# A two-layer attention trunk: memory's normalization factor is applied behind the key and value products

## The chip, the cores and the metric

The kernel runs on one core of a Trainium2 chip. The core has five engines with a queue each: TensorE (PE, matrix products; its loads of the stationary operand are shown as PEld), VectorE (DVE), ScalarE (ACT), GpSimd (POOL) and SyncE (SP, which issues most transfers). An engine works through its queue in order and waits on semaphores for the others. The metric is the time of one execution on the device in microseconds (us), as the median of several. Before the change it is 966.31 us (three runs, 966.08 to 968.67).

## The reference

The reference is a trunk of two layers over 512 tokens of width 1024, with 256 memory tokens of the same width. The part that matters here is the attention into memory, which each layer does with its own weights over the same memory:

```python
def rmsnorm(x, g):
    xf = x.astype(jnp.float32)
    y = xf * lax.rsqrt(jnp.mean(xf * xf, axis=-1, keepdims=True) + EPS)
    return (y * g.astype(jnp.float32)).astype(x.dtype)
...
    mem_h = rmsnorm(mem, mem_norm_g[i])
...
    kv = jnp.einsum('bnd,de->bne', mem_h, w_kv).reshape(Bn, N, 2, MEM_HEADS, HEAD_DIM)
    k = rmsnorm(kv[:, :, 0], kn_g)
    v = kv[:, :, 1]
```

A row of `mem` is divided by its root mean square (one number per memory token, here called its factor), multiplied by a row of 1024 gains, and multiplied with the weights of key and value. The keys are normalized once more, per head of 128. `x` goes through an `rmsnorm` of its own in each layer, and then through a wide input projection, a token mixer (dilated windows in layer 0, grouped queries in layer 1), the memory attention, a gate, and an output projection that is added to `x`.

## The kernel before

**Products in three parts.** Each f32 operand is split into a high part in the rounded format of TensorE (`wh` for weights, `act`, `h` for activations; ScalarE copies it) and the rest (`wo`; VectorE subtracts it, L305 and L161). A product is high times high and low times high (L170, L171, `mm_early`), then high times low weights (L174, `mm_late`). Four blocks of 128 rows give eight early and four late products, called a group.

**Weights.** `Weights` holds the loads in one list in the order of use. `W.dma` issues loads of 512 KB on SP while buffers are free, `W.hi` makes ScalarE's copy (L295), `W.lo` VectorE's subtraction (L305). Four buffers each of `wh` and `wo` turn round.

**Order.** The program is written out by hand: Python calls issue each instruction onto its engine's queue. A `Driver` holds side tasks as generators: after each group of products `drv.tick` lets those run a step that are due. `chunk` runs groups: it takes the weights, calls `group` for each block of rows, then frees banks, advances the weights and ticks. So side tasks stand behind the group that was issued just before.

**The start (from L885).** SP loads memory's gain row (4 KB), x's gain row (4 KB), two blocks of memory (512 KB each) with weights between, the gain columns, and four blocks of x with more weights. TensorE spreads both gain rows over the 128 partitions by multiplying a column of ones with them (`row_bank`, L606): four products, two passes each. The squares of a memory block run on ScalarE and, for one half of the first block, VectorE (`norm_1`); POOL adds them, adds epsilon and raises to −1/2 (L477, L436, L437). VectorE multiplies by factor and gain row (`norm_2`, L482). TensorE transposes four squares of 128 (`turn4`, L488), ScalarE copies the high part, VectorE subtracts the low one. `mid` puts a small product (`busy`) and work on the weights between. `ahead`, called ahead of each group, transposes the remaining quarters of memory and copies x's gain row from its bank.

**Key and value (`mem_kv`).** Two `proj_t` chunks: keys with two units of weights by two blocks of memory tokens, then values. The keys' `ev_k` squares the heads on ScalarE (L573), takes the factor per head on POOL (L436, L437), multiplies on VectorE (L578), transposes (L585) and writes both parts (L633, L634). The values' `ev_v` writes both parts with a constant 0.5 (L656, L657). Beside the keys and values the side task `prep` normalizes and transposes x: `norm_1` on ScalarE and POOL, L482 on VectorE, L488 on TensorE, copies and differences for the products of the first large projection, which follows.

**The second layer.** `mem_norm(1)` is a side task during the output projection of layer 0. It loads memory again, computes the factor again, scales and transposes. `mem_kv(1)` follows the output projection, while the new x is normalized.

## Time and profile before

| what | value |
|---|---|
| median of three runs | 966.31 us |
| the profiled execution | 968.3 us |
| its span, first to last instruction | 966.5 us |
| TensorE busy | 946.8 us, 98% |
| VectorE busy | 791.4 us, 82% |
| ScalarE busy | 681.7 us, 71% |
| GpSimd busy | 341.4 us, 35% |
| mean granted TensorE clock | 0.996 |

The numbers come from one execution that the hardware profiler recorded. Times in its rows are us from the start of the span. A row of the timeline has start, duration, engine, source line, operation, output and inputs with their shapes, a count when several are merged, and in brackets how long the engine had stood idle and what ended that. A row of the chain of waits has start, duration, and what the chain consists of there. A row of the windows has the stretch, its length, then busy us with the number of instructions for PE, PEld, DVE, ACT and POOL, the granted TensorE clock, the busy share of the transfer engines and GB/s. A row of the groups has the shape, the busy us in all, and the mean ns of one.

### The profile page before, as it was taken

The page shows a single profiled execution, that of the slowest core. Times are in us where ns is not written, and L with a number is a line of the kernel's source. Part 1 is how long each engine was busy: PE and PEld are TensorE (multiplying, and loading weights), DVE is VectorE, ACT ScalarE, POOL GpSimd, SP SyncE. Part 2 cuts the span into 40 slices and gives each one's busy share as a digit, 9 for nine tenths or more (in the row PEclk, how much of TensorE's full clock was granted, in tenths as well). Part 3 has the DMA queues.
Part 4 walks back from the last instruction along what each step waited for, and adds up shares of the span by engine and source line. Part 5 has one row for each costly group of instructions (what it writes and reads, how often), then busy time and mean ns, then how long its engine had stood idle before and what let it go on. Part 6 is the DMA issues. An engine that isn't in the chain of part 4 may idle for free.

```text
span 966.5 us, 16604 instructions
## 1 busy us (share of the span) xinstructions
PE 946.8 (98%) x5682; PEld 833.2 (86%) x5682; DVE 791.4 (82%) x1411; ACT 681.7 (71%) x1701; POOL 341.4 (35%) x482
## 2 busy tenths in 40 slices
PE   8999999999999999999999999999899999999998
PEld 5879888888888888888899997788899999998886
DVE  5898676878888888888888999769878898769883
ACT  5775689686868686868685657546768977879770
POOL 1512423557554545454726011322332330111010
PEclk9999999999999999999999999999899999999999
DMA  9989956969686868685959889889766687777744
GB/s 360 317 235 327 271 116 172 294 120 268 149 258 143 262 150 258 154 261 132 283 132 241 266 206 297 268 242 366 167 157 129 199 235 179 207 204 190 206 131 131
DMA packets 89129, 209.81 MB, mean 217 GB/s; under 512 B 25298, under 2 KB 36050, under 8 KB 89044
## 3 DMA queue, kind: packets, MB, share of 16 engines
q1 hardware_dynamic: 69892, 145.76, 43.4%
q0 software_dynamic: 17856, 60.83, 33.4%
q10 hardware_dynamic: 1296, 2.16, 0.6%
q8 instruction: 45, 0.74, 0.3%
q14 instruction: 40, 0.33, 0.1%
HBM read 157.27 MB, written 12.65 MB: 176 GB/s over the span
## 4 chain that ended last, share of the span: by engine, by line
PE 80%; DVE 8%; DMA 6%; ACT 3%; issue 2%; POOL 1%; SPq 0%; DVEq 0%; POOLq 0%; ACTq 0%
PE pj L170 21%; PE pj L171 21%; PE pj L174 20%; DVE wo L305 2%; PE qT L585 2%; PE sa L1106 1%; PE oo L1208 1%; PE pt L1187 1%; PE sa L1102 1%; PE ptb L1405 1%; DMA og<-odb 1%; DMA acc<-sn 1%; DMA wl<-wl 1%; DMA grB<-in_qn_b_dram 1%; DMA od<-o 1%
## 5 line engine op out<-in xcount | busy, mean ns | idle before, releaser
L305 DVE TENSOR_TENSOR wo<-wl,wh 128x1024 fp32r<-128x1024 f32 x255 | 315.1, 1242 | 6.0 <-ACT wh L295 5.8
L295 ACT CAST wh<-wl 128x1024 fp32r<-128x1024 f32 x255 | 268.5, 1060 | 29.3 <-PE pj L171 18.9
L170 PE MATMUL pj<-wh,hS 128*128 128x512 f32 (+1 forms) x448 | 159.0, 368 | 3.9 <-DVE sn L389 3.9
L171 PE MATMUL pj<-wh,hS 128*128 128x512 f32 (+1 forms) x448 | 153.6, 356 | 0.0
L170 PE MATMUL pj<-wh,h 128*128 128x512 f32 (+1 forms) x336 | 117.9, 365 | 0.0
L171 PE MATMUL pj<-wh,h 128*128 128x512 f32 (+1 forms) x336 | 114.0, 353 | 0.0
L437 POOL TENSOR_TENSOR rstd<-mse,half 128x4 f32<-128x4 f32 (+2 forms) x98 | 103.1, 1052 | 8.2
L174 PE MATMUL pj<-wo,hS 128*128 128x512 f32 (+1 forms) x448 | 100.8, 355 | 2.0 <-DVE wo L305 2.0
L170 PEld LDWEIGHTS pj<-wh,hS 128*128 128x128 f32 x448 | 85.9, 192 | 14.8 <-issue 2.6
L171 PEld LDWEIGHTS pj<-wh,hS 128*128 128x128 f32 x448 | 86.1, 192 | 10.3
L372 ACT COPY sn<-pj 128x512 f32<-128x512 f32 x132 | 73.1, 590 | 29.7 <-PE pj L174 29.7
L436 POOL TENSOR_SCALAR mse<-hss 128x4 f32<-128x4 f32 (+1 forms) x86 | 45.1, 525 | 132.2 <-ACT junk L573 128.0
L174 PEld LDWEIGHTS pj<-wo,hS 128*128 128x128 f32 x448 | 75.3, 191 | 14.5 <-DVE wo L305 2.7
L573 ACT ACTIVATE junk<-sn 128x128 f32<-128x128 f32 x264 | 79.1, 308 | 4.1 <-DVE sn L383 4.1
L1050 POOL TENSOR_TENSOR ta<-sn,tabs 128x128 f32<-128x128 f32 (+1 forms) x64 | 37.4, 592 | 118.6 <-DVE sn L578 92.0
L389 DVE TENSOR_TENSOR sn<-pj,sn 128x512 f32<-128x512 f32 x99 | 67.7, 686 | 12.3 <-PE pj L174 11.8
L174 PE MATMUL pj<-wo,h 128*128 128x512 f32 (+1 forms) x336 | 74.8, 352 | 0.0
L171 PEld LDWEIGHTS pj<-wh,h 128*128 128x128 f32 x336 | 63.8, 190 | 7.4
L170 PEld LDWEIGHTS pj<-wh,h 128*128 128x128 f32 x336 | 63.6, 189 | 7.4 <-DVE sn L389 0.2
L279 POOL DMA_DIRECT2D wl<-wl x33 | 29.1, 881 | 111.9 <-DVE wo L305 56.0
L174 PEld LDWEIGHTS pj<-wo,h 128*128 128x128 f32 x336 | 56.0, 189 | 8.7
L578 DVE TENSOR_TENSOR sn<-sn,rstd 128x512 f32<-128x512 f32 (+1 forms) x82 | 48.0, 594 | 7.2 <-POOL rstd L437 7.2
(235 smaller groups left out, 2335.1 us busy)
## 6 DMA issues: line engine op xcount, KB each, us to landing
wl<-in_wall_dram SPq DMA_DIRECT2D x222, 512.0 KB, 7.0
wl<-wl POOLq DMA_DIRECT2D x66, 512.0 KB, 5.5
wl<-in_wall_dram POOLq DMA_DIRECT2D x42, 512.0 KB, 8.5
acc<-sn POOLq DMA_DIRECT2D x16, 256.0 KB, 4.8
od<-o SPq DMA_DIRECT2D x12, 256.0 KB, 5.6
og<-od SPq DMA_DIRECT2D x12, 256.0 KB, 5.5
odb<-o SPq DMA_DIRECT2D x12, 256.0 KB, 3.4
og<-odb SPq DMA_DIRECT2D x12, 256.0 KB, 4.2
```

The costliest lines, as they stand in the source:

```text
L170: T.matmul(o, a, b, start=start, stop=False, skip_group_check=True)
L171: T.matmul(o, c, d, start=False, stop=False, skip_group_check=True)
L174: T.matmul(o, a, b, start=False, stop=stop, skip_group_check=True)
L295: A.copy(wh, self.tile[self.items[i]])
L305: V.tensor_tensor(wo, self.tile[key], wh.bitcast(F32), ALU.subtract)
L372: A.copy(t, b)
L389: V.tensor_tensor(t, b, t, ALU.subtract if q == "12" else ALU.add)
L436: G.tensor_scalar(e, ss, EPS, None, ALU.add)
L437: G.tensor_tensor(r, e, half[:, 0:n], ALU.pow)
L573: A.activation(jk, p[:, j * 128:(j + 1) * 128], AF.Square, scale=QS, accum_out=ss[:, j:j + 1])
L578: V.tensor_tensor(xn[:, 0:n], p.rearrange("p (a b) -> p a b", a=4)[:, 0:n], r[:, 0:n, None].to_broadcast([128, n, 128]), ALU.mult)
L1050: G.tensor_tensor(ta[:, 0:n], xn[:, 0:n, 0:32], ropeA[:, 0, b, s0:s0 + n], ALU.mult)
```

## The change

Memory's rows are multiplied by the gain row alone and transposed; the factor of a row is applied behind the products, where each memory token is a partition again. Three columns hold it: the factor itself, the factor times 128^-1/2 for the squares of the key heads, and half of it for the values. For the keys, the head factor from POOL is multiplied once more (`G.tensor_scalar(r, r, rm[0]...)`), since the product lacks the row's factor. Layer 1 uses the columns that layer 0 left, since memory is the same, and computes no squares.

x's gain row is no longer spread by TensorE and copied by ScalarE, but loaded to all 128 partitions by a transfer of 512 KB. One product of a row of zeros (`idle`, `IDLE = 1`) stands ahead of memory's row products, and the small product `busy` is gone. The order of the first loads changes: two weight loads between the memory blocks.

The hook that `proj_t` calls moves from ahead of a group (`pre`) to between its early and late products (`mid`), and what `ahead` does moves a group earlier. The high part of the very first transposed quarter is copied by VectorE.

```diff
-    def proj_t(act, sels, evac, pre=None):
+    def proj_t(act, sels, evac, mid=None):
         def group(w, u, b, p):
             for k in range(4):
                 kk = 4 * u + k
                 mm_early(p, sels[b](act, 0, kk), w[k][0], sels[b](act, 1, kk), w[k][0], kk == 0)
+            if mid:
+                mid(u, b)
             for k in range(4):
...
-    def head_sq(p, n=4):
+    def head_sq(p, n=4, by=QS):
...
-            A.activation(jk, p[:, j * 128:(j + 1) * 128], AF.Square, scale=QS, accum_out=ss[:, j:j + 1])
+            A.activation(jk, p[:, j * 128:(j + 1) * 128], AF.Square, scale=by, accum_out=ss[:, j:j + 1])
...
+    def mem_mul(xb, row, j):
+        t = s2(name="mg")
+        V.tensor_tensor(t, xb[j], row[j], ALU.mult)
+        return t
+    def mem_turn(M, t, b, j):
+        cs = slice(b * 128, (b + 1) * 128)
+        turn4(t, M.block(0, j, cs), M.block(1, j, cs))
+    def mem_factor(b, ss):
+        e = sm(1, "mse")
+        G.tensor_tensor(e, ss[:, 0:1], ss[:, 1:2], ALU.add)
+        r = rstd_of(e, 1)
+        for k, by in enumerate((1.0, QS, 0.5)):
+            G.tensor_scalar(rm[k][:, b:b + 1], r, by, None, ALU.mult)
+    def mem_rows(layer):
...
         yield MEM_D
-        n = [norm_1(t[0])]
-        yield 1
-        n.append(norm_1(t[1]))
-        norm_2(t[0], n[0], rows["m"])
-        yield 1
-        norm_2(t[1], n[1], rows["m"])
         M = Act(NM)
         for b in range(2):
+            g = [mem_mul(t[b], rows["m"], j) for j in range(2)]
+            yield 1
             for j in range(2):
-                norm_3(t[b], M, b * 128, j)
+                mem_turn(M, g[j], b, j)
             yield 1
...
-            r = head_sq(p)
+            r = head_sq(p, by=rm[1][:, b:b + 1])
             def rest():
+                G.tensor_scalar(r, r, rm[0][:, b:b + 1], None, ALU.mult)
                 xn = head_mul(p, r)
...
-            A.activation(vt_[0][:, b], p, AF.Copy, scale=0.5)
-            V.scalar_tensor_tensor(vt_[1][:, b], p, 0.5, vt_[0][:, b].bitcast(F32), ALU.mult, ALU.subtract)
+            A.activation(vt_[0][:, b], p, AF.Copy, scale=rm[2][:, b:b + 1])
+            V.scalar_tensor_tensor(vt_[1][:, b], p, rm[2][:, b:b + 1], vt_[0][:, b].bitcast(F32), ALU.mult, ALU.subtract)
...
-    for b in range(2):
-        nc.sync.dma_start(mt[b], mem[b * 128:(b + 1) * 128])
-        W.dma(1)
+    nc.sync.dma_start(mt[0], mem[0:128])
+    W.dma(2)
+    nc.sync.dma_start(mt[1], mem[128:256])
     W.dma(2)
...
         nc.sync.dma_start(xt[c], xv[c])
+        if c == 0:
+            row_load("x", norm_g[0:1, :])
...
-    first = row_bank("m0", WARM)
-    gain = row_bank("x0", 1, pj)
...
+    idle = tabs[0:1, 512:1024]
+    V.memset(idle, 0.0)
+    for n in range(IDLE):
+        T.matmul(at("idle"), ones, idle, start=True, stop=True)
+    first = row_bank("m0")
...
+    mg = {(0, 0): mem_mul(mb[0], first, 0)}
+    square(0, 0)
+    square(0, 1, True)
+    p = turn4(mg[0, 0], None, None)
+    hi, lo = M.block(0, 0, slice(0, 128)), M.block(1, 0, slice(0, 128))
+    split(hi, lo, p, False)
     W.hi(True)
+    W.lo()
     W.hi(True)
-    norm_2(mb[1], nst[1], first, (0,))
+    mg[1, 0] = mem_mul(mb[1], first, 0)
     W.lo()
+    mem_factor(0, ss[0])
     def ahead(u, b):
+        if (u, b) == (0, 0):
+            mem_turn(M, mg[1, 0], 1, 0)
+            for c in range(2):
+                mg[c, 1] = mem_mul(mb[c], first, 1)
+                square(1, c)
+            mem_factor(1, ss[1])
         if (u, b) == (0, 1):
-            for j in range(2):
-                A.copy(rows["x"][j], gain[j])
-            norm_3(mb[1], M, 128, 0)
             for c in range(2):
-                norm_2(mb[c], nst[c], first, (1,))
-        if (u, b) == (1, 0):
-            for c in range(2):
-                norm_3(mb[c], M, 128 * c, 1)
+                mem_turn(M, mg[c, 1], c, 1)
...
-    drv.spawn(mem_norm(1), MEM_B)
+    drv.spawn(mem_rows(1), MEM_B)
```

In the queues this gives, after the first low operand: on ScalarE the two weight casts of the second unit of the keys and the first squares of x now stand behind the last two copies of memory's transposed quarters; on POOL the extra multiplication for the first key block stands behind the norm of the third x block, that for the second behind the fourth's.

More of the change, by code (lines that the diff above doesn't have):

```diff
@@ L27 @@
 MEM_D = 4
+IDLE = 1
 PD = 2
@@ L944, in setup, with square @@
             yield 1
[L946 to L964 removed]
+    idle = tabs[0:1, 512:1024]
[3 more added lines that the diff above has]
+    first = row_bank("m0")
+    mb, M = [halves(t) for t in mt], Act(NM)
+    ss = [sm(2, "ss") for _ in range(2)]
+    def square(b, j, vector=False):
+        jk = s2(name="sq")
+        if vector:
+            V.tensor_tensor_reduce(jk, mb[b][j], mb[b][j], 1.0 / 1024.0, 0.0, ALU.mult, ALU.add, ss[b][:, j:j + 1])
+        else:
+            A.activation(jk, mb[b][j], AF.Square, scale=1.0 / 32.0, accum_out=ss[b][:, j:j + 1])
+    mg = {(0, 0): mem_mul(mb[0], first, 0)}
[4 more added lines that the diff above has]
+    split(hi, lo, p, False)
+    W.hi(True)
+    W.lo()
     W.hi(True)
[L966 removed]
+    mg[1, 0] = mem_mul(mb[1], first, 0)
     W.lo()
+    mem_factor(0, ss[0])
     def ahead(u, b):
+        if (u, b) == (0, 0):
[4 more added lines that the diff above has]
+            mem_factor(1, ss[1])
         if (u, b) == (0, 1):
[L972 to L974 removed]
             for c in range(2):
[L976 to L979 removed]
+                mem_turn(M, mg[c, 1], c, 1)
     drv.spawn(prep(), PD)
```

27 lines of the change are left out of this document (6 added, 21 removed).

## The prediction

> **What bounds the kernel.** I read the page first, then the chain of waits in order of time, then the timeline of each engine where the change works, the windows, and the groups by form.
>
> ```profile
> span 966.5 us, 16604 instructions
> PE 946.8 (98%) x5682; PEld 833.2 (86%) x5682; DVE 791.4 (82%) x1411; ACT 681.7 (71%) x1701; POOL 341.4 (35%) x482
> ...
> 2.26 7.16 PE row L606 x8
> 9.41 1.04 PE xT L488 x4
> ...
> 11.18 0.75 PE pj L170
> ...
> 12.65 0.43 PE pj L170
> ...
> 14.36 0.25 PE pj L170
> ```
>
> TensorE is busy 98% of the span, so nothing between the two ends of the change can give time. What can give or cost is where TensorE stands: the start (first product at 11.18, eight passes of row products, 7.16 us, ahead of it) and the places where another engine sets its pace. A product takes 0.43 us at 12.65 and 0.25 from 14.36 on: the clock comes up at about 14.3.
>
> ```profile
> 31.00:40.00 9.00, 9.00 (x51) 7.72 (x50) 9.00 (x13) 6.86 (x20) 5.47 (x7) 1.00 0.90 314
> 50.00:60.00 10.00, 9.78 (x42) 7.51 (x42) 9.84 (x15) 8.67 (x13) 2.29 (x3) 1.00 0.93 175
> ...
> 29.85 1.29 DVE L161 TENSOR_TENSOR h<-xT,h 128x512 fp32r<-128x512 f32 x2 [1.00 <-ACT h L158]
> 61.85 0.68 DVE L389 TENSOR_TENSOR sn<-pj,sn 128x512 f32<-128x512 f32 x1
> 62.59 0.50 PE L170 MATMUL pj<-wh,hS 128*128 128x512 f32 x1 [1.43 <-DVE sn L389]
> ```
>
> In the windows (behind the length stand TensorE, its loads, VectorE, ScalarE and POOL) VectorE has no gap from 31 on. At 62.59 TensorE stands 1.43 us for it. So TensorE's lead at the start is spent there: the time at 62.59 is that of VectorE's queue, which began at 29.85, when ScalarE had copied the first transposed x block.
>
> ```profile
> 16.72 2.00 ACT L295 CAST wh<-wl 128x1024 fp32r<-128x1024 f32 x2
> 18.62 0.63 ACT L475 ACTIVATE sq<-x 128x512 f32<-128x512 f32 x1
> 20.89 1.08 ACT L158 CAST act<-xT 128x512 fp32r<-128x512 f32 x2 [0.93 <-PE xT L488]
> 21.85 2.01 ACT L295 CAST wh<-wl 128x1024 fp32r<-128x1024 f32 x2
> 23.75 0.64 ACT L475 ACTIVATE sq<-x 128x512 f32<-128x512 f32 x1
> 25.08 0.28 ACT L573 ACTIVATE junk<-pj 128x128 f32<-128x128 f32 x1
> 26.10 2.01 ACT L295 CAST wh<-wl 128x1024 fp32r<-128x1024 f32 x2
> ...
> 29.22 1.08 ACT L158 CAST h<-xT 128x512 fp32r<-128x512 f32 x2
> ```
>
> ScalarE has no gap from 20.89 to 29.22. It starts this run when the last transposition of memory is done (the pair, 20.89): two weight casts, squares of an x block, head squares, two casts, squares, and then the copy that VectorE waits for, 8.33 us later.
>
> **Part 1, the start.** Four of the eight row passes go (x's norm row), two idle ones come: six by 7.16/8 = 0.895 are 5.4 us. The idle product waits for a memset of 512 elements on one partition, between one and four times the 128-element one below; I take 0.6, and so a start at 1.6.
>
> ```profile
> 0.84 0.17 DVE L450 MEMSET tabs<- 1x128 f32 x1
> L1191 DVE COPY pT<-pt 128x512 f32<-128x512 f32 x8 | 5.5, 690 | 0.0
> ```
>
> Transpositions then start at 7.0 against 9.41. The scaling that waited for squares and POOL is a plain product, done under the row passes. The upper copy moves to VectorE (0.69, the second row): first product 7.0 + 1.04 + 0.7 = 8.8, that is 2.4 us earlier. Its low part follows 0.7 later.
>
> Six more products of the group run to 12.7 at 0.43. The next transpositions stand ahead of the low products, not behind them, so ScalarE's copy and VectorE's subtraction lie beside four products. If the clock comes up at 14.3 as before, the pair begins at 17.2; if it comes up as long after the first product as before (3.1 us, so 11.9), at 16.2. I take 16.7, 4.2 us earlier than 20.89.
>
> **Part 2, ScalarE's order.** Gone from its queue ahead of the pair: two copies of x's row and one upper copy. But the casts of 16.72 and the squares of 18.62, which filled its wait, now stand behind the pair: 18.62 − 16.72 = 1.90, and 25.08 − 23.75 = 1.33 for squares. The four head squares take their factor from a column.
>
> ```profile
> L633 ACT ACTIVATE kmT<-qT,gc 128x512 fp32r<-128x512 f32 x4 | 2.7, 686 | 0.0
> L656 ACT ACTIVATE vm<-pj 128x512 fp32r<-128x512 f32 x4 | 2.4, 592 | 0.0
> L634 DVE SCALAR_TENSOR_TENSOR kmT<-qT,gc,kmT 128x512 fp32r<-128x512 f32 x4 | 3.0, 747 | 0.0
> L657 DVE SCALAR_TENSOR_TENSOR vm<-pj,vm 128x512 fp32r<-128x512 f32 x4 | 2.8, 691 | 0.8 <-ACT vm L656 0.8
> ```
>
> A column as scale costs ScalarE 686 − 592 = 94 ns and VectorE 56 ns against a constant. So pair to copy is 8.33 + 1.90 + 1.33 + 4 × 0.094 = 11.9 us: the copy starts at 28.6 against 29.22, 0.6 earlier. Of 4.2 us on TensorE that much reaches VectorE.
>
> **Part 3, the factor behind the products.** Per key block POOL gets one multiplication, which the scaling of the heads on VectorE (L578 before) waits for. In the queue it stands behind the norm of the next x block.
>
> ```profile
> 32.88 1.21 POOL L436 TENSOR_SCALAR mse<-hss 128x4 f32<-128x4 f32 x1 [2.00 <-ACT junk L573]
> 36.91 0.57 POOL L437 TENSOR_TENSOR rstd<-mse,half 128x1 f32<-128x1 f32 x1
> 37.58 0.69 DVE L578 TENSOR_TENSOR xn<-pj,rstd 128x512 f32<-128x512 f32 x1
> 658.91 0.26 POOL L436 TENSOR_SCALAR mse<-hss 128x4 f32<-128x4 f32 x1 [4.36 <-ACT junk L573]
> ```
>
> For the second block POOL was through at 37.48, just ahead of 37.58. It begins 0.6 earlier by the copy and 0.4 later by the head squares, so it ends at 37.3; the multiplication, of the shape of L436, costs 0.26 (VectorE idle) to 1.21 (VectorE at work). VectorE stands while it waits, so I take 0.3, near the row where it stood: 37.7 with the hand-over, where the queue would be at 37.0. Of the gain of 0.6 the wait takes 0.7, and what is queued behind it on VectorE waits along: sums of weights, the next x block, low parts of weights, and through them TensorE at 62.59. Value's two low parts (0.056 each) and the ScalarE write ahead of the second (0.094) add 0.2. Start in sum: +0.3 us, +0.8 with the pair at 17.2, up to +1.7 with that and the multiplication at 1.21; −0.2 with the pair at 16.2.
>
> The factor's own operations on POOL, three more columns a block, lie ahead of the first norm of x, which waits for ScalarE: nothing, and without that cover three times 0.3.
>
> **Part 4, x's row by transfer.** A 512 KB transfer stands in SP's queue ahead of three x blocks and the weights; 4 KB go.
>
> ```profile
> 22.00:24.00 2.00, 1.77 (x9) 1.44 (x9) 2.00 (x4) 2.00 (x3) 0.14 (x1) 1.00 1.03 422
> 11.51 13.89 SPq L246 DMA_DIRECT2D wl<-in_wall_dram  x12
> wl<-in_wall_dram SPq DMA_DIRECT2D x2, 512.0 KB, 10.9
> ```
>
> At 422 GB/s it costs 1.2 us for each load behind it. The weights issued at 11.5 land by about 22.4, 23.6 then; their cast was at 26.10 and comes at 25.5 (20.89 to 26.10 is 5.21, plus 3.6, from 16.7). 1.9 us of slack hide it; without that slack the cast and the whole run behind it would wait up to 1.2.
>
> **Part 5, the second layer.** Four squares on ScalarE, six POOL operations and the factor in four VectorE products go.
>
> ```profile
> 600.00:640.00 40.00, 39.03 (x192) 32.15 (x191) 30.79 (x41) 19.31 (x33) 9.07 (x12) 1.00 0.85 258
> 661.21 1.29 DVE L161 TENSOR_TENSOR h<-xT,h 128x512 fp32r<-128x512 f32 x2 [2.13 <-ACT h L158]
> 664.57 1.06 PE L488 MATMUL xT<-ident,acc 128*128 128x128 f32 x8 [1.32 <-DVE acc L482]
> 679.68 0.69 DVE L657 SCALAR_TENSOR_TENSOR vm<-pj,vm 128x512 fp32r<-128x512 f32 x1 [0.38 <-ACT vm L656]
> 685.25 0.55 PE L170 MATMUL pj<-wh,hS 128*128 128x256 f32 x1 [2.47 <-DVE sn L389]
> ```
>
> They lie under TensorE, busy 39.03 of 40 us there: nothing won, and the output products are the cover. From 661 on VectorE again sets the pace until 685.25. ScalarE runs head squares, casts and the copy for 661.21 without a gap, so 4 × 0.094 = 0.4 land whole; vm adds 0.2 as above. The second layer costs 0.6.
>
> **Sum:** +0.3 + 0.6 = +0.9 us. The profiled execution took 968.3 us, 1.8 more than its span, and becomes 969.2. It stands 2.0 above the median, 966.31; on that the forecast is 967.2.
>
> **The rivals.** One: TensorE's start counts in full, because VectorE has room I don't see. For it: the first product is 2.4 earlier, the pair 3.7 at the same clock; against it: the rows without gaps. 966.3 − 2.4 + 0.6 = 964.5, or 963.2 with 3.7. It needs a pair so early that ScalarE's longer queue behind it no longer decides, before about 15.
>
> Two: the row and idle products, from 1.6 on, bring the clock up before the first product. Against it: 7.16 us of row products on one partition did not raise it here, a product after them still took 0.43. If they did: with 0.25 in place of 0.43 the seven products between 8.8 and 11.9 take 1.3 less, and the pair starts at 16.2 − 1.3 = 14.9 at best, 1.8 earlier than I take: 965.4. The Trainium skill, "TensorE: Matmul & The Clock Gate", Part 1: The HAM clock gate, says that some 3.4 us of sustained matmuls bring the full clock. By that the full clock should stand here from about 9 us at the latest (an estimate from that page, two of its windows behind 2.26); the trace, with 14.3, disagrees for such products, and no run here shows why.
>
> Three, slower: the multiplication runs while VectorE is at work and is held as the same shape is here.
>
> ```profile
> 687.29 3.11 POOL L436 TENSOR_SCALAR mse<-hss 128x4 f32<-128x4 f32 x1 [13.93 <-ACT junk L573]
> ```
>
> At 3.11 instead of 0.3 in both blocks it adds up to 2 × 2.8: 970.0 for one, 972.8 for both. It decides from about 2 us a block on. Against it: VectorE is waiting for just this.
>
> Four: the half-clock stretch around 685 changes. TensorE stands 2.47 us there and then works at a granted clock of 0.50.
>
> ```profile
> 683.40:690.00 6.60, 4.75 (x22) 4.78 (x23) 6.60 (x9) 3.80 (x13) 2.71 (x1) 0.50 0.38 104
> ```
>
> Of 4.75 busy us half is the price, 2.4; a shift of the work against the stretch can give that or cost as much again: 964.8 to 969.6.
>
> **How the numbers follow.** Forecast 0.58 (966.7 to 968.6), one 0.12, two 0.10, three 0.10, four 0.10. A measurement of this kernel tells about 0.3%, 2.9 us, from no change: below 963.4 or above 969.2. Faster 0.06: part of one, a little of two and four. Slower 0.16: three, and 0.06 from four and the forecast's upper end. The rest, 0.78, is within. The range reaches from 964.5 (one) to 969.8 (below three).
>
> **What would show it.** First product near 8.8, pair near 16.7 and ScalarE without a gap from there to the h copy at 28 to 29; VectorE's first h subtraction within 1 us of 29.85; a wait of VectorE for POOL at the second key block; TensorE's stand at 62.59 grown by the lead it has won. In the second layer 661.21 and 685.25 later by 0.4 and 0.6 against the work before. Wrong, if TensorE passes the VectorE stand earlier by more than 1.5 us, if POOL holds VectorE over 2 us, or if weights land late at 25.

## The result: 0.4% slower, and the profile after

The changed kernel took 971.0 us (median of 8, 968.33 to 972.67) and the kernel before 967.62 us (8, 966.08 to 969.89) side by side: a ratio of 1.0037, 95% interval 1.0024 to 1.0050. That is +3.4 us where +0.9 was forecast, and 971.0 lies above the range's 969.8. In every later set the kernel before stood between 967.3 and 968.0. The profiled execution of the changed kernel took 972.64 us, 970.7 of them span. One execution of a later run, `after_order`, took 1561.59 us at a granted clock of 0.559 and is left out of its ratio.

Two words are used throughout: an engine stands while it is idle and waits for something, and a transfer lands when its data have arrived.

In the changed kernel's file VectorE's scaling of the heads is L580 (L578 before), POOL's norm L435 and L436 (L436 and L437), its new multiplication L662, the products L171, L172 and L175 (L170, L171, L174), ScalarE's head squares L575 (L573).

First the start, from the timeline of the changed kernel (start, duration, engine, line, operation, and in brackets how long the engine had stood and for what):

```profile
1.60 2.07 PE L966 MATMUL idle<-tabs 1*128 1x512 f32 x2 [1.60 <-DVE tabs L964]
7.02 1.11 PE L488 MATMUL xT<-ident,mg 128*128 128x128 f32 x4
9.01 0.76 PE L171 MATMUL pj<-wh,act 128*128 128x512 f32 x1 [0.88 <-DVE act L161]
...
17.61 1.08 ACT L159 CAST act<-xT 128x512 fp32r<-128x512 f32 x2 [1.90 <-PE xT L488]
...
29.31 1.08 ACT L159 CAST h<-xT 128x512 fp32r<-128x512 f32 x2
29.93 1.29 DVE L162 TENSOR_TENSOR h<-xT,h 128x512 fp32r<-128x512 f32 x2 [1.00 <-ACT h L159]
...
37.72 0.32 POOL L662 TENSOR_SCALAR rstd<-rstd,rm 128x4 f32<-128x4 f32 x1
38.07 0.69 DVE L580 TENSOR_TENSOR xn<-pj,rstd 128x512 f32<-128x512 f32 x1 [0.16 <-POOL rstd L662]
...
63.30 0.50 PE L171 MATMUL pj<-wh,hS 128*128 128x512 f32 x1 [1.40 <-DVE sn L388]
```

TensorE's first product is 2.2 us earlier than the 11.18 of before. ScalarE's copy of the pair (memory's last two transposed quarters) is 3.3 us earlier (17.61, 20.89), but its copy of x that VectorE waits for is 0.1 us later (29.31, 29.22). TensorE stands at 63.30 where it stood at 62.59. This place moves by itself: it lies between 62.59 and 64.22 in the eleven traces of this study whose start is not the changed one, and between 62.53 and 63.58 in the nine where it is. So the start is level: what TensorE won at 9 is gone at 63.

Next the second layer's keys, POOL, VectorE and TensorE by time, before:

```profile
664.60 1.04 POOL L437 TENSOR_TENSOR rstd<-mse,half 128x4 f32<-128x4 f32 x1
664.94 2.36 DVE L305 TENSOR_TENSOR wo<-wl,wh 128x1024 fp32r<-128x1024 f32 x2
665.60 0.95 POOL L274 DMA_DIRECT2D wl<-in_wall_dram  x1
667.21 0.69 DVE L578 TENSOR_TENSOR xn<-pj,rstd 128x512 f32<-128x512 f32 x1
681.56 1.22 PE L174 MATMUL pj<-wo,hS 128*128 128x256 f32 x8 [1.81 <-DVE wo L305]
```

and after:

```profile
664.29 2.14 POOL L436 TENSOR_TENSOR rstd<-mse,half 128x4 f32<-128x4 f32 x1
664.31 2.35 DVE L306 TENSOR_TENSOR wo<-wl,wh 128x1024 fp32r<-128x1024 f32 x2
666.39 0.96 POOL L275 DMA_DIRECT2D wl<-in_wall_dram  x1
667.07 0.65 POOL L662 TENSOR_SCALAR rstd<-rstd,rm 128x4 f32<-128x4 f32 x1
667.76 0.69 DVE L580 TENSOR_TENSOR xn<-pj,rstd 128x512 f32<-128x512 f32 x1 [1.09 <-POOL rstd L662]
682.31 1.55 PE L175 MATMUL pj<-wo,hS 128*128 128x256 f32 x8 [2.70 <-DVE wo L306]
```

POOL's norm of the second key block takes 2.14 us where it took 1.04, then POOL issues a weight transfer, and only behind it comes the new multiplication. VectorE, which had no wait for POOL there, stands 1.09 us. TensorE at 682 stands 2.70 us, and 2.70 to 2.72 in all nine traces of kernels that place the multiplication like this. With the old second layer it stood 1.11 to 1.84 us (eight traces).

Last, 230 us behind the last changed instruction, the gate of the last layer. From the chain of waits (start, duration, what), before:

```profile
903.17 6.68 DMA og<-odb
910.04 0.51 issue
910.55 0.68 DVE nmb L1385
911.30 0.59 DVE pbT L1414
911.89 0.61 DVE sn L389
912.54 0.50 PE pj L170
```

and after:

```profile
898.72 5.81 DMA odb<-o
904.67 0.38 SPq L798
905.10 0.46 SPq L886
905.60 0.43 SPq L886
906.08 6.64 DMA og<-odb
...
914.76 0.61 DVE sn L388
915.41 0.79 PE pj L171
```

`o`, the attention's output, is stored to memory (`odb`) and loaded again in two parts (`og`). SP issues the loads when the store has landed, and between the two loads it issues two transfers of 512 KB for the output projection (L886). The store was issued at the same time (898.66 before, 898.72 after) and the last load takes the same (6.68, 6.64), but the store landed in 5.8 us where it had needed 3.0:

```profile
wl<-in_wall_dram SPq DMA_DIRECT2D x4, 512.0 KB, 4.4
odb<-o SPq DMA_DIRECT2D x2, 256.0 KB, 3.0
```

These are the median times to landing from 879 to 912 before, and after:

```profile
wl<-in_wall_dram SPq DMA_DIRECT2D x4, 512.0 KB, 6.3
odb<-o SPq DMA_DIRECT2D x2, 256.0 KB, 5.8
```

The weights that SP loads from 880 on land later too, and with them POOL's two accumulating loads, which need a buffer of theirs, are issued later. From the timelines before

```profile
892.29 0.87 POOL L274 DMA_DIRECT2D wl<-in_wall_dram  x1 [7.57 <-PE sb L166]
912.54 0.50 PE L170 MATMUL pj<-wh,yS 128*128 128x512 f32 x1 [0.74 <-DVE sn L389]
```

and after:

```profile
894.71 0.87 POOL L275 DMA_DIRECT2D wl<-in_wall_dram  x1 [9.87 <-DVE rdb L1415]
915.41 0.79 PE L171 MATMUL pj<-wh,yS 128*128 128x512 f32 x1 [3.61 <-DVE sn L388]
```

So 6.4 us lay between the first of them and the store, and 4.0 lie there now: the accumulating loads run beside the store. (The engines that the brackets name had long been done; it is the landing that POOL waits for.) TensorE's stand grows from 0.74 to 3.61 us, and it takes up work at half its clock (0.79 us against 0.50). In the windows TensorE's granted clock is 0.51 from 915.00 to 918.50, and in the kernel before it stays at 1.00 there:

```profile
915.00:918.50 3.50, 3.09 (x7) 2.48 (x8) 3.50 (x7) 3.09 (x7) 0.86 (x1) 0.51 0.92 215
```

At half the clock this costs some 1.5 us (an estimate, half of the 3.09 busy us of the row). The page of before had this transfer in its line of the chain, "DMA og<-odb 1%" of the span; the prediction did not quote it.

The loss lies here in the other traces too. From TensorE's product at 878 (`ob`, 878.00 before and 878.11 after) to the last instruction pass 88.5 us before and 92.6 after. With the late transfers as they are, it is 87.4 to 89.5 in nine traces whose start is not the changed one (mean 88.3) and 89.0 to 92.6 in six with the changed start (mean 90.6). Three of the six have the half clock behind the stand (stands of 2.12, 2.32 and 3.61 us), and one with a stand of 2.60 does not.

Two theories came out of this. The second layer's multiplication costs what it does by its place; and the start, level itself, changes how the transfers of the last gate fall. The rival of each is told with its runs.

### The profile page after: what moved, and what is told of

Its sections match the earlier page's. It is cut to its first block, busy times and chain, and to the rows that moved or that the text cites. A ratio compares the mean times of both kernels' runs of the same rounds, so it can differ in the third digit from the quotient of the medians.

```text
span 970.7 us, 16589 instructions
## 1 busy us (share of the span) xinstructions
PE 946.6 (98%) x5678; PEld 832.8 (86%) x5678; DVE 792.8 (82%) x1413; ACT 679.4 (70%) x1690; POOL 341.5 (35%) x486
## 4 chain that ended last, share of the span: by engine, by line
PE 84%; DVE 7%; DMA 4%; ACT 2%; issue 1%; POOL 1%; SPq 0%; DVEq 0%; ACTq 0%; POOLq 0%
PE pj L171 22%; PE pj L172 22%; PE pj L175 21%; PE qT L587 2%; DVE wo L306 2%; PE sa L1129 1%; PE oo L1231 1%; DMA od<-o 1%; PE pt L1210 1%; PE ptb L1428 1%; PE sa L1125 1%; PE xT L488 1%; PE ob L175 1%; DMA wl<-in_wall_dram 1%; PE pmt L732 1%
## 5 line engine op out<-in xcount | busy, mean ns | idle before, releaser
L171 PE MATMUL pj<-wh,hS 128*128 128x512 f32 (+1 forms) x448 | 159.0, 368 | 4.6 <-DVE sn L388 3.5
L172 PE MATMUL pj<-wh,hS 128*128 128x512 f32 (+1 forms) x448 | 153.4, 355 | 0.0
L171 PE MATMUL pj<-wh,h 128*128 128x512 f32 (+1 forms) x336 | 117.9, 364 | 0.0
L172 PE MATMUL pj<-wh,h 128*128 128x512 f32 (+1 forms) x336 | 114.0, 353 | 0.0
L436 POOL TENSOR_TENSOR rstd<-mse,half 128x4 f32<-128x4 f32 (+2 forms) x96 | 100.8, 1050 | 8.0
L175 PE MATMUL pj<-wo,hS 128*128 128x512 f32 (+1 forms) x448 | 100.6, 354 | 2.9 <-DVE wo L306 2.9
L171 PEld LDWEIGHTS pj<-wh,hS 128*128 128x128 f32 x448 | 85.9, 192 | 15.9 <-issue 2.4
L172 PEld LDWEIGHTS pj<-wh,hS 128*128 128x128 f32 x448 | 86.0, 192 | 10.2
L435 POOL TENSOR_SCALAR mse<-hss 128x4 f32<-128x4 f32 (+1 forms) x86 | 46.1, 536 | 128.6 <-ACT junk L575 124.4
L175 PEld LDWEIGHTS pj<-wo,hS 128*128 128x128 f32 x448 | 75.1, 191 | 15.3 <-DVE wo L306 3.5
L575 ACT ACTIVATE junk<-sn 128x128 f32<-128x128 f32 x264 | 79.1, 308 | 4.5 <-DVE sn L382 4.5
L388 DVE TENSOR_TENSOR sn<-pj,sn 128x512 f32<-128x512 f32 x99 | 67.5, 684 | 11.9 <-PE pj L175 11.4
L175 PE MATMUL pj<-wo,h 128*128 128x512 f32 (+1 forms) x336 | 74.8, 352 | 0.0
L172 PEld LDWEIGHTS pj<-wh,h 128*128 128x128 f32 x336 | 63.7, 190 | 7.5
L171 PEld LDWEIGHTS pj<-wh,h 128*128 128x128 f32 x336 | 63.6, 189 | 7.5 <-DVE sn L388 0.2
L175 PEld LDWEIGHTS pj<-wo,h 128*128 128x128 f32 x336 | 56.0, 189 | 8.8
L580 DVE TENSOR_TENSOR sn<-sn,rstd 128x512 f32<-128x512 f32 (+1 forms) x82 | 47.8, 592 | 7.7 <-POOL rstd L436 7.7
```

Of the source, the lines that this page charges most:

```text
L171: T.matmul(o, a, b, start=start, stop=False, skip_group_check=True)
L172: T.matmul(o, c, d, start=False, stop=False, skip_group_check=True)
L175: T.matmul(o, a, b, start=False, stop=stop, skip_group_check=True)
L388: V.tensor_tensor(t, b, t, ALU.subtract if q == "12" else ALU.add)
L435: G.tensor_scalar(e, ss, EPS, None, ALU.add)
L436: G.tensor_tensor(r, e, half[:, 0:n], ALU.pow)
```

## Experiments

**The halves.** `start_only` is the changed kernel with the second layer as before; `second_only` and `second_pad` are the kernel before with the changed second layer (`second_pad` with the new small tile padded to 64 bytes, so that the buffers behind it stay aligned as before; both make the factor columns at the start, by six small operations on POOL); `after_again` is the changed kernel once more.

```diff
# start_only, from the changed kernel
-    drv.spawn(mem_rows(1), MEM_B)
+    drv.spawn(mem_norm(1), MEM_B)
# second_only, from the kernel before
-            r = head_sq(p)
+            r = head_sq(p, by=rm[1][:, b:b + 1]) if layer else head_sq(p)
...
+                if layer:
+                    G.tensor_scalar(r, r, rm[0][:, b:b + 1], None, ALU.mult)
...
-    drv.spawn(mem_norm(1), MEM_B)
+    drv.spawn(mem_rows(1), MEM_B)
```

> The changed kernel once more, without an edit, for a second trace of it. Theory A (tail): the 3.4 us of the median come from one place, TensorE's stand near 915 us for the last gate (3.61 us against 0.74), behind it four products at half clock; up to 878 us the two kernels are level (878.11 against 878.00). Expected: median 970 to 972, again +1.2 us against the kernel before at its product of 593.67 and less than 0.5 at 878.00; the time of the profiled execution follows the stand near 915: about 967 + the stand + 1 where the stand is over 2 us. Rival B (start): the median is slower because of the start and the second layer; the stand near 915 comes and goes in both kernels and adds to neither in the mean. Then this trace shows over 2 us of loss ahead of 878, or a stand near 915 under 1 us with a time over 970.

> The changed kernel with the second layer's memory work as it was before (normalized ahead of the products, constant factors), the start as changed. Theory A: at the product of 593.67 it is 1.0 to 1.4 us later than the kernel before, as the changed kernel is, and its end depends on the stand near 915: anything from 967 to 971.5. If the second layer gives the 1.1 us back that the traces show between 622 and 878, this run is 0.5 to 1.5 us later than the kernel before at 878. Rival B: the start costs most of the 3.4: 969.5 to 971.5, with at least 2 us of it visible ahead of 650.

> The kernel before with the second layer's memory work alone as changed (gain row only ahead of the products, columns as factors; the columns made from layer 0's factors by six small GpSimd operations at the start), the columns' tile 64 bytes wide so that no buffer moves off its multiple of 64. Prediction on record: +0.6 us for this layer, 966.9 to 968.5. By the traces of the changed kernel the second layer is 0.5 to 1 us shorter between 594 and 686 than before: 966 to 967. By C nothing else shows; by D nothing either, since the start is the old one.

> The second layer's change alone once more, the tile of columns at its 24 bytes as in the changed kernel; where the buffers start made no difference (967.29 for the shifted kernel before). Theory E (the second layer costs by itself): 1 to 2 us over the kernel before, as the first such run (969.39 against 967.55) and the differences of the pairs say (971.0 - 969.56 between the changed kernel and its start alone; 968.1 - 966.4 between the two kernels with the later loads); 968.5 to 969.5. Rival: that was scatter, and it is 0.5 over at most: 967 to 968.

| run | median us | before beside it | ratio, 95% interval | stand at 682 | stand at 912 |
|---|---|---|---|---|---|
| after_again | 970.95 | 967.3 | 1.0031, 1.0016 to 1.0046 | 2.71 | 1.41 |
| start_only | 969.56 | 967.3 | 1.0021, 1.0004 to 1.0037 | 1.84 | 2.12 |
| second_pad | 969.39 | 967.55 | 1.0017, 1.0001 to 1.0032 | 2.70 | 0.43 |
| second_only | 969.98 | 968.04 | 1.002, 1.0004 to 1.0036 | 2.71 | 0.17 |

(The stands are those of the one profiled execution of each. The ratio is not exactly the quotient of the two medians.) By the medians the start alone costs 2.3 us and the second layer alone 1.8 to 1.9; 4.1 to 4.2 together, against 3.4 to 3.7 measured for both. The intervals are wide: each of the halves may cost from next to nothing to some 3.5 us. Each half has one of the two stands and not the other.

**The late loads ahead of the bulk.** In the last output projection the 512 KB transfers are issued one group of products later, so that both loads of `og` stand ahead of them in SP's queue; in the changed kernel, in the one before, and in the padded changed one.

```diff
-    def out_proj(YW, ys, src, evac, tiles, half=False):
+    def out_proj(YW, ys, src, evac, tiles, half=False, acc_at=ACC_AT):
...
-        drv.spawn(load(), ACC_AT)
+        drv.spawn(load(), acc_at)
...
-    out_proj(YW, ys, x1d, ev_o2, acc_b, HALF.get("o"))
+    out_proj(YW, ys, x1d, ev_o2, acc_b, HALF.get("o"), 5)
```

> The changed kernel with the loads of the last sum (acc<-x1d, 4 x 512 KB) started one group later in layer 1: on SP's queue both gate loads (og<-odb) then stand ahead of them, nothing else moves. Theory A: the second gate load no longer shares the transfers with 1 MB that stands ahead of it; it lands within about 3 us of its issue, as the first one did (2.6 us), not 6.64; the stand near 915 falls from 3.61 to under 1 us and the four half-clock products go: 971.0 - 2.9 - 1.3 = 966.8, range 966 to 968.5. Rival B: the stand was not what makes the median slower: 970 to 971.

> The kernel before with the same edit of SP's queue. Theory A: its stand near 912 is small (0.74 in its trace, probably larger in its slower executions): 966 to 967, and the difference of the two kernels with this edit is 0 to 0.6 us instead of 3.4. Rival B: the difference stays 2.5 to 3.4 us with the edit in both.

> The changed kernel with the 64-byte tile of columns and with the last loads of x1d a group later in SP's queue. Theory C: level with the kernel before with that queue edit (966.4) within 0.7: 965.7 to 967.1, the fastest kernel so far if the second layer's half microsecond counts. Rival D: 968.5, as without the padding.

`after_acc5` 968.53 us (1.0015, 1.0001 to 1.003), 2.4 below the changed kernel in the same set; `before_acc5` 966.4 (0.9983, 0.9968 to 0.9999), 0.9 below the kernel before; `after_pad_acc5` 967.6 (1.0001, 0.9989 to 1.0012). TensorE stands for `sn` at 912 in none of the three, though the store of `after_acc5` still takes 4.8 us. What the order wins in the changed kernel beyond what it wins in the one before, 1.5 us (3.0 in the padded pair, 971.5 to 967.6), is loss by the wait for the second load and the half clock behind it. From 878 to the end all traces with this order take 87.2 to 87.4 us, with either start, so nothing of the start's loss is left there. `after_acc5` is still 2.1 us behind `before_acc5`, where 0 to 0.6 was expected; by the halves that is the second layer. `before_acc5` has the lowest median of this study.

**The delay by itself.** Four small multiplications on POOL ahead of the two accumulating loads, in the kernel before. Nothing of the change is in it.

```diff
+                    if c == SEQ[-3] and x == 0:
+                        for _ in range(4):
+                            jk = small.tile([128, 128], F32, tag="junk", name="junk", bufs=2)
+                            G.tensor_tensor(jk, self.tile[key][:, 0:128], self.tile[key][:, 128:256], ALU.mult)
```

> The kernel before with the first of the two late accumulating loads (the pair that GpSimd issues at 892.29 and 893.53) held back by four small GpSimd multiplications on its target buffer (their results are not used), 128x128 each, 0.58 us by the row of that shape: about 2.3 us later, the difference that separates the two kernels there (892.29 and 894.71, counted from 878.00 and 878.11). Theory A (tail): the pair then runs beside the store of 898.66, the store lands 1.5 to 2.8 us later than its 3.0, the stand near 912 grows from under 1 to 1.4 to 3.6 us, and the time by 1 to 3: 968.5 to 970.5. Against it: the store lands in 3 us all the same, and the time stays at 967 to 968; then the late pair only goes along with a stand that something else makes.

972.49 us (six executions), 1.0051 (1.0034 to 1.0069): as slow as the changed kernel or slower, and 2 us above what was expected at most. From its landing times, POOL's and TensorE's timeline:

```profile
odb<-o SPq DMA_DIRECT2D x2, 256.0 KB, 5.3
...
891.89 2.70 POOL L277 TENSOR_TENSOR junk<-wl 128x128 f32<-128x128 f32 x4 [7.76 <-DMA wl<-in_wall_dram]
894.95 1.79 POOL L278 DMA_DIRECT2D wl<-in_wall_dram  x2 [0.36 <-POOL junk L277]
...
914.09 0.50 PE L170 MATMUL pj<-wh,yS 128*128 128x512 f32 x1 [2.88 <-DVE sn L393]
```

Accumulating loads issued 3.1 us ahead of the store (898.08 in this run) make it land in 5.3 us and TensorE stand 2.88 us; the half clock follows (0.50 at 916 to 918), and from 877.41 to the end pass 92.1 us, near the 92.6 of the changed kernel. This chain is shown, from the loads on.

**What in the start delays the loads.** Seven runs took one difference each: where the buffers lie (`after_pad`, `before_shift`, both by 32 bytes), x's row by the 512 KB transfer (`before_row512`), which buffers the weights fall into (`before_h2`, `after_h2`), and the order of the first loads (`before_order`, `after_order`).

```diff
# after_pad
-    rm = pool.tile([128, 6], F32, name="rm").rearrange("p (k b) -> k p b", k=3)
+    rm = pool.tile([128, 16], F32, name="rm")[:, 0:6].rearrange("p (k b) -> k p b", k=3)
# before_shift
-    half = pool.tile([128, 8], F32, name="half")
+    half = pool.tile([128, 16], F32, name="half")[:, 0:8]
# before_row512
+            row_load("x", norm_g[0:1, :])
...
-            for j in range(2):
-                A.copy(rows["x"][j], gain[j])
# before_h2 and after_h2
+    spare = m4(name="row1")[0:1, :]
+    V.memset(spare[:, 0:1], 0.0)
# before_order; after_order is its reverse
-    for b in range(2):
-        nc.sync.dma_start(mt[b], mem[b * 128:(b + 1) * 128])
-        W.dma(1)
+    nc.sync.dma_start(mt[0], mem[0:128])
+    W.dma(2)
+    nc.sync.dma_start(mt[1], mem[128:256])
```

> The changed kernel with one edit: the new tile of factor columns is 64 bytes wide per partition instead of 24. In the changed kernel it takes 32 bytes, so every buffer behind it (weights, memory, x, stores, sums) starts 32 bytes later than in the kernel before: the first weight buffer at 11040 instead of 11008, 32 bytes past a multiple of 64; with 64 bytes it starts at 11072, a multiple of 64 again. No instruction changes place. Theory C (alignment): transfers into and out of buffers off a multiple of 64 take longer, which is why, near 888 us, the two weight loads land in 6.3 us in all four traces with the new tile and in 4.0 and 4.3 in the two without, the accumulating loads behind them then run beside the store, and TensorE stands 1.4 to 3.6 us. Expected by C: those loads land in about 4.2 us, the store within 3.1, the stand near 912 is under 1 us, and the time is 966.5 to 968. Rival D (order of transfers or turn of buffers): the 512 KB row in place of 4 KB, or the one buffer less, shift the turns; then padding does nothing: 6.3 us, 970 to 971.5.

> The kernel before with one edit: the tile of constants that lies ahead of the buffers (half) is 64 bytes wide instead of 32, of which 32 are used; every buffer behind it starts 32 bytes later (11040), as in the changed kernel. No instruction changes. Theory C: the two weight loads near 888 land in about 6.3 us instead of 4.0 to 4.3, the stand near 912 grows to 1.4 to 3.6 us, and the time goes up by 2 to 3.5: 969 to 971. Rival D: no difference, 966.5 to 968.

> The kernel before with x's gain row loaded by the 512 KB transfer behind the first x block, in place of the 4 KB load and ScalarE's two copies (TensorE still does the four row products, now of memory's row, and nobody reads them). The number of transfers is the same. Theory D1 (history of the transfers): the longer list of packets at the start changes how the transfers near 880 are served for good; GpSimd's pair comes 10.4 to 10.8 us behind its copy of 883.9 (after: 10.74, before: 8.42), the stand near 912 is 1.4 to 3.6, 968.5 to 970.5. If the row's transfer has no part in it: 8.4 us, and 967 to 968, or up to 1 us less since ScalarE is two copies shorter at 11.9.

> The kernel before with one more 4 KB buffer taken at the start and given back after the first products (two memsets of one element on VectorE): the transfers and their order stay, but 266 of the 330 weight loads go to other buffers than in the kernel before. Theory D2 (which buffers the transfers use): the gap of 8.42 us between GpSimd's copy and its pair near 892, and with it the stand near 912 and the time, move to other values than before: a gap of 10 or more and 968.5 to 971 would be the pattern of the changed kernel. Theory D1: gap 8.3 to 8.8, 967 to 968.

> The changed kernel with the same extra buffer: transfers and order as in the changed kernel, 282 of the 330 weight loads to other buffers. Theory D1: the gap stays at 10.4 to 10.8 and the time at 970 to 971.5. Theory D2: the gap can fall to about 8.4, the stand near 912 with it, and the time to 967.5 to 969.

> The kernel before with the first loads on SP's queue in the order of the changed kernel (two weight loads between the two memory blocks); nothing else moves. Theory D3 (order of the first loads): the turn in which the transfer engines serve SP's and GpSimd's queues is set at the start and kept; then SP's load behind the store of 880 is issued in 0.33 us, as in all traces with the changed start (1.1 to 1.6 in those with the old one), GpSimd's pair comes 10.4 to 10.8 behind its copy, the stand near 912 is over 1.4, and the time is 969 to 971. Against it: 1.1 to 1.6, gap 8.3 to 9.2, 967 to 968.

> The changed kernel with the first loads in the order of the kernel before (memory, weight, memory, three weights). Theory D3: issue 1.1 to 1.6, gap 8.3 to 9.2, stand near 912 under 1, and 968 to 969.5. Against it: issue 0.33, gap 10.4 to 10.8, 970 to 971.5.

The last column is the wait of POOL ahead of the loads: from its last transfer between two weight buffers (`wl<-wl`, near 884) to the first of the two that add weights from memory (near 892 or 894), one trace each.

| run | median us | ratio, 95% interval | POOL's last `wl<-wl` to its first accumulating load, us |
|---|---|---|---|
| after_pad | 971.5 | 1.0038, 1.002 to 1.0056 | 10.60 |
| before_shift | 967.29 | 0.9999, 0.9985 to 1.0014 | 8.33 |
| before_row512 | 967.97 | 1.0006, 0.9993 to 1.002 | 9.17 |
| before_h2 | 968.17 | 1.0003, 0.9987 to 1.0019 | 8.30 |
| after_h2 | 971.05 | 1.004, 1.0026 to 1.0054 | 10.70 |
| before_order | 967.57 | 1.0001, 0.9982 to 1.0021 | 8.34 |
| after_order | 972.76 | 1.0036, 1.0019 to 1.0052 | 10.47 |

None moves the kernel to the other side: the old start keeps 8.3 to 9.2 us and its time, the changed one 10.5 to 10.7 and its loss (8.42 and 10.74 in the two kernels themselves). So none of these single differences is the cause by itself. Two of them together, and the rest of the new start (the product of zeros, the moved hook, VectorE's copy), were not run, and what makes the weights land later at 880 stays open. (`second_mul`, below, has the late landing in its trace without that start.)

**The multiplication's place.** In `second_mul`, POOL multiplies by memory's factor right behind the head norm and no longer behind the transfer it issues. `second_nofac` leaves the factor out in the second layer. `after_acc5_mul` is the changed kernel with this place and with the late loads ahead.

```diff
# second_mul, from second_only
             r = head_sq(p, by=rm[1][:, b:b + 1]) if layer else head_sq(p)
+            if layer:
+                G.tensor_scalar(r, r, rm[0][:, b:b + 1], None, ALU.mult)
...
-                if layer:
-                    G.tensor_scalar(r, r, rm[0][:, b:b + 1], None, ALU.mult)
# second_nofac, from second_only: neither of the two, and
-            by = rm[2][:, b:b + 1] if layer else 0.5
+            by = 0.5
```

> The kernel before with the second layer of the change alone, as measured at 969.98 against 968.04 (1.002), but POOL's multiplication by memory's factor is issued right behind the head norm, ahead of the transfer that POOL issues, and no longer behind it. Theory Q (the second layer costs what it does because the multiplication stands in POOL's queue behind the issue of a transfer, 0.96 us, and is then held itself): VectorE's wait of 1.1 us for POOL at 667 to 668 falls to under 0.4, TensorE's stand of 2.71 us at 682 falls to 1.8 or less, and the time to 968.3 to 969.2, 0.8 to 1.6 below the form measured. Rival R (the cost is the norm itself, 2.14 us with VectorE at work where it took 1.04 with VectorE idle, and the squares, 0.37 each for 0.28): the multiplication only moves, VectorE still waits 0.7 or more, the stand stays at 2.4 to 2.8 and the time at 969.5 to 970.3.

> The second layer of the change alone, but the factor of memory's rows is left out there altogether: the keys' squares and the values take constants as scale, as in the kernel before, and POOL gets no multiplication (the second layer's keys and values then lack the factor). What is left of the change is that memory's rows are not normalized a second time. Theory Q or R (the operations that carry the factor cost 1.9 us): the stand at 682 goes back to 1.1 to 1.8 us, and the time to that of the kernel before or up to 0.5 below it (967.5 to 968.3). Rival S (the work removed under the output projection moves something there, and that costs): the stand stays at 2.7, and the time at 969.5 to 970.3.

> The changed kernel with both mends: in the last output projection the two late loads stand ahead of the 512 KB accumulations (measured before at 968.53 and 967.6 against 967.3 and 967.55), and in the second layer POOL's multiplication stands right behind the head norm. If theory Q holds and the two add up: 0.8 to 1.6 below the changed kernel with the first mend alone, so 966.3 to 967.6 where the kernel before has 967.5, a ratio of 0.999 to 1.000. Rival R: 967.6 to 968.6, a ratio of 1.000 to 1.0015.

`second_mul` took 967.77 us beside 967.85 (1.0001, 0.9979 to 1.0022), `second_nofac` 966.7 (0.9989, 0.9973 to 1.0005), `after_acc5_mul` 967.46 (0.9993, 0.9978 to 1.0008). From the timelines, `second_mul`:

```profile
664.05 2.13 POOL L437 TENSOR_TENSOR rstd<-mse,half 128x4 f32<-128x4 f32 x1
664.07 2.35 DVE L305 TENSOR_TENSOR wo<-wl,wh 128x1024 fp32r<-128x1024 f32 x2
666.28 0.31 POOL L672 TENSOR_SCALAR rstd<-rstd,rm 128x4 f32<-128x4 f32 x1
666.62 0.69 DVE L579 TENSOR_TENSOR xn<-pj,rstd 128x512 f32<-128x512 f32 x1 [0.21 <-POOL rstd L672]
681.18 1.22 PE L174 MATMUL pj<-wo,hS 128*128 128x256 f32 x8 [2.00 <-DVE wo L305]
```

and `second_nofac`:

```profile
663.01 1.04 POOL L437 TENSOR_TENSOR rstd<-mse,half 128x4 f32<-128x4 f32 x1
663.36 2.35 DVE L305 TENSOR_TENSOR wo<-wl,wh 128x1024 fp32r<-128x1024 f32 x2
665.62 0.68 DVE L579 TENSOR_TENSOR xn<-pj,rstd 128x512 f32<-128x512 f32 x1
679.96 1.21 PE L174 MATMUL pj<-wo,hS 128*128 128x256 f32 x8 [1.13 <-DVE wo L305]
```

The norm in `second_mul` is held as in the changed kernel (2.13), the multiplication falls from 0.65 (in `second_only`) to 0.31 and has no issue ahead of it, and VectorE's wait goes from 1.11 to 0.21. The stand at 682 falls by 0.7, and the ratio from 1.002 to 1.0001, 1.8 us, though with intervals as wide as that. The wait and the time fit theory Q and not R; the stand, 2.00, lies between them (1.8 or less, and 2.4 or more). What is left of it over 1.13 are the norm that is held and the longer squares, so R has a part too. `second_nofac` has the norm at 1.04, no wait and a stand of 1.13, so the removed work under the output projection costs nothing (rival S falls), and the operations that carry the factor are the whole loss of this layer. Its time is 0.8 us below what was expected; the interval still includes the kernel before. `after_acc5_mul` has no stand at 912, 0.21 and 2.01 at the two places of the second layer, and the time of the kernel before: the two causes account for the loss within the interval. Against the kernel before with its loads ahead (0.9983) it is 0.1% behind, less than these runs can tell; it is no faster kernel.

## Why the prediction was wrong

**The bound.** "TensorE is busy 98% of the span, so nothing between the two ends of the change can give time. What can give or cost is where TensorE stands": the rule was right and its list was short. It held the start and the second layer, which the edit touches, and left out the stand at 912, which waits for a chain of transfers and had 0.74 us of it already in the trace of before. This is the step that failed first, and the larger of the two: it put the start at +0.3 by the stand at 62.59, and the start cost 2.3 us by `start_only`, 1.5 us by the order of the loads, at a place 850 us later. No rival had it. That a change at the start would reach the transfers of the last gate could not be worked out from the trace of before; that this place had no slack could.

**Part 1** held by its mechanism. First product 9.01 (8.8), products of the group 0.43 apart to 12.8 (12.7). The pair is at 17.61 (16.7, at most 17.2): ScalarE stood 1.90 us for the transpositions, which TensorE began at 16.97, behind all eight early products of the second group. The products reached their fast length at about 14, as before (0.69 to 0.39 us in the four low products from 13.50 on), which by the prediction gives 17.2. The rest is a wait that it had put at nothing, for the low part of the second group: VectorE wrote it from 14.51 to 15.20, and the product behind the one at 14.73 came at 15.26, 0.3 late. The granted clock in the windows is 1.00 over all of this stretch in both kernels, so the pace is read from the lengths of the products alone.

**Part 2** held: 11.70 us from the pair to the copy (11.9), head squares of 0.37 where they were 0.28 (+0.094 each). The 0.9 by which the pair came late is why the copy is at 29.31 and not 28.6.

**Part 3** held. The multiplication took 0.32 us (0.3), VectorE waited 0.16 for it, and its scaling began at 38.07 where it had begun at 37.58. The start's +0.3 can't be told from the level start that was measured. One reading under it was wrong: at 658.91, the row of 0.26, VectorE was not idle but at work on two operands until 659.08 (0.69 us from 658.39), so "idle" and "at work" do not part 0.26 from 1.21.

**Part 4** held: ScalarE's run from 17.61 to 29.31 has no gap, so no weights came late, and `before_row512` has a ratio of 1.0006 (0.9993 to 1.002).

**Part 5** is the second step that failed, by a size: +0.6, where 1.8 to 1.9 were measured (0.6 is still inside the interval of each run alone; the place is shown by the traces, where TensorE's stand at 682 grows by 0.9 to 1.6). It counted ScalarE's squares and the values' operations and no multiplication on POOL at all; Part 3's price of 0.3 was taken at the start alone. The mechanism stood in rival three, in one block and not in both, at some 1.1 us by VectorE's wait and not 2.8, and with another cause than the row of 3.11 suggested: it is POOL's norm that is held, and the multiplication stands behind an issue of 0.96 us. The sentence against that rival, "VectorE is waiting for just this", was true of the multiplication itself at 667.07 (VectorE stood from 666.67 on, and it took 0.65) and passed over the norm ahead of it, which ran beside VectorE's subtraction from 664.31 on. The squares, priced at 0.4 us, have a hand in that: being longer, they let the norm begin only 0.02 us ahead of that subtraction, where it began 0.34 ahead before. `second_nofac` and `start_only`, with a constant for these squares, have 0.35 and 0.34, and 1.04 for the norm.

**The other rivals.** Rival one fell, since TensorE at 63 is where it was. Rival two fell: TensorE worked on one-partition products from 1.60 on, and the products behind them were still 0.43 apart at 12.4; the first of the fast length came at about 14. Rival four had no part that a run shows: from 594 to 686 executions with the same second layer differ by up to 3.5 us (88.8 to 92.3 with the old one), and the time of one pair of traces says nothing about it. In the pair shown here that stretch is 0.4 us shorter after the change, while the timings of the halves say 1.9 longer.

## What to carry to other kernels

List every place in the whole span where the bound engine stands, those that wait for transfers too, with the slack of each, before a change is called local: work moved at one end can come out at the other. Price an added operation at each place where it is issued, by what stands ahead of it in its queue there and by what the engine beside it is doing then. Where two transfers of one queue are wanted at different times, put the small one that somebody waits for ahead of the bulk: that was worth 0.9 us before the change and 2.4 after.

## What was not expected of the hardware

A POOL norm of 512 numbers takes 1.04 us when it begins 0.34 us ahead of VectorE's subtraction of two operands (664.60 and 664.94, 663.01 and 663.36; nine traces), and 2.13 to 2.14 when both begin within 0.02 us (ten traces; 3.27 in an eleventh, `after_h2`). The Trainium skill, "SBUF — State Buffer", Who interferes with whom, says that a VectorE instruction with two inputs in that memory contends with a POOL instruction that reads it, and that the order of issue decides who waits. The rows agree as to the contention; as to the order they show POOL held though it begins 0.02 us ahead, so the begin in the trace does not settle it.

The store of 256 KB near 898 lands in 2.1 to 3.1 us when the first of two accumulating loads was issued 5.6 us or more ahead of it, in 3.8 when it was 5.0, and in 4.3 to 5.8 when it was 4.4 or less. The Trainium skill, "DMA: Bandwidth & Descriptors", Issuing engines are not separate DMA queues, says that transfers of all issuers run on the same engines and interleave; the rows agree with that.

From POOL's `wl<-wl` near 884 to its first accumulating load, which waits for a landing, pass 8.3 to 9.2 us in nine traces whose start is not the changed one and 10.4 to 10.8 us in eight with the changed start, though both issue the same transfers there. (In `before_pooldelay` its small multiplications, which wait for the same landing, begin after 8.62.) Two traces do not fit: `second_mul`, with the old start, has 10.56 and a stand of 1.89 at 912, and `after_acc5_mul`, with the new one, 9.74. Both place the second layer's multiplication elsewhere. So the changed start is not needed for the late landing, and one trace a kernel cannot tell how often it comes. What decides it is open.
